# An output projection's left half ranked ahead of the last attention block, and weight casts queued behind a copy

## The chip, the cores and the metric

The kernel runs on one core of a Trainium2 chip. The metric is the device time of one execution in microseconds. The core's engines work from queues of their own: TensorE (PE, matrix products and transposes), ScalarE (ACT), VectorE (DVE), GpSimd (POOL), and SyncE (SP), from which most loads are issued.

## The reference

One decoder layer on a sequence of 1024 tokens, width 1024, in float32:

```python
z = h @ w_in                                  # columns: [pool group | q | k | v]
y_pool = pool_mixer(u_pool, w_pool, pool_scale)   # causal means over 2, 4, 8, 16 tokens, minus the token, a map per group
y_attn = sliding_window_attention(q, k, v, sinks) # window 128, 8 query heads, 2 key heads, blocks of 128 queries
mix = concat([y_pool, y_attn]) @ w_out
h = layer_norm(ALPHA * h + mix, ln1_g, ln1_b)
ff = square(relu(h @ w_ff1)) @ w_ff2
h = layer_norm(ALPHA * h + ff, ln2_g, ln2_b)
h = h + sigmoid(h @ w_ple_gate + b) * (p @ w_ple)
```

## The kernel before

Every product is made of three: each operand is split into a high part (a cast by ScalarE, `high`, L98) and a low part (the difference, `low`, L103, by VectorE or GpSimd), and `mm3` adds high x high (L112), high x low (L113) and low x high (L114) in one PSUM bank.

The tokens are worked on in two halves of 512 (t = 0, 1), in eight blocks of 128. `z_tile` makes 128 columns of z for one half. The first three (keys, values, first query) are made by `z_first`. `values` copies its product to SBUF (L238), transposes it on TensorE (L241) and splits it. `queries(t, half)` loads and splits the weights of two tiles of queries, multiplies, and evicts (L260, L261). `attention(n)` does one block: for each of the two key groups two score tiles (L288, L289, into banks of the tag "s", of which there are two), a reduction against bias and sinks by VectorE (L292), exponentials by ScalarE (L299) behind a small copy of the sinks by GpSimd (L297), the scaling (L305), transposes (L312), and products with the values (L317, L318), added up at L321. `pooling` makes the pooling groups: a product of z in a bank "mm" (three of them), its copy (L348), sums on GpSimd (L356), the difference on VectorE (L359), its split into the tile tmp, and a product with `wp` in another bank "mm", evicted at L374 and L375.

`out_left(t, ...)` multiplies the four blocks of a half with the left 512 columns of w_out: eight k steps, four blocks, three products each, 96 in all. Four accumulators are taken for all of it: three banks "mm" and one "s". The weights come in four pieces of two k steps through two tiles "w", each cast by ScalarE and, in the first half, finished by GpSimd. `residual_left` adds the accumulators to the residual (L436), which `residual_load` has fetched. `out_right(n)` does the right columns of a block, with weights kept in two large tiles, in one bank "mm".

The order in which each engine issues is not written out by hand. A planner in the framework lays out the whole program before it runs: where several instructions could go, the one that is earlier in the program goes first, by planned times; an instruction that isn't ready is passed over. `tc.issue_after(i)` puts all that is traced within it, on the engine of i, behind i. So the place of a call in the program is a rank, and not a place in time. The calls around the edits stand at L471 to L491 and L588 to L600.

Of the kernel before, what the change touches and what calls it, by code (L numbers as in the profile page):

```python
# [12 lines left out]
P = 128  # L13
D = 1024
S = 1024
HALF = 512
# [51 lines left out]
def layer(ctx, tc, xT, x, pT, w_in, w_pool, pscale, sinks, w_out, ln1, w1, w2, ln2, w_ple, w_gate, bgate, bias, rcount, out):  # L68
    nc = tc.nc
# [6 lines left out]
    def nm(s):  # L76
        uid[0] += 1
        return f"{s}_{uid[0]}"
# [4 lines left out]
    def wt(shape, dt=F32R):  # L83
        return sb.tile(shape, dt, tag="w", bufs=2, name=nm("w"))

    def nat(shape, dt=F32):
        return sb.tile(shape, dt, tag="n", bufs=8, name=nm("n"))

    def stage(shape):
        return sb.tile(shape, F32, tag="st", bufs=2, name=nm("st"))  # L90
# [5 lines left out]
    def high(dst, src, scale=None):  # L96
        if scale is None:
            nc.scalar.copy(out=dst, in_=src)  # L98
        else:
            nc.scalar.mul(out=dst, in_=src, mul=scale)  # L100

    def low(eng, dst, src, hi):
        return eng.tensor_tensor(out=dst, in0=src, in1=hi.bitcast(F32), op=ALU.subtract)  # L103
# [38 lines left out]
    def keep(shape, dt=F32R):  # L142
        return pa.tile(shape, dt, tag="k", bufs=3, name=nm("k"))
# [4 lines left out]
    def row(shape, dt=F32):  # L148
        return pa.tile(shape, dt, tag="h", bufs=6, name=nm("h"))
# [14 lines left out]
    def acc_ps():  # L164
        return ps.tile([P, HALF], F32, tag="mm", bufs=3, name=nm("mm"))

    def tr_ps():
        return ps.tile([P, 4, P], F32, tag="pt", bufs=2, name=nm("pt"))
# [13 lines left out]
    def z_tile(c, t, home=None):  # L182
        w = (home or wt)([P, 2, NK, P])
        load_split(w[:, 0], w[:, 1], w_in[c], [P, NK, P], nc.vector)
        o = acc_ps()
        for k in range(NK):
            z_mm(o, w, t, k)
        return o
# [3 lines left out]
    def z_first():  # L192
        w = [wt([P, 2, NK, P]) for _ in range(2)] + [big([P, 2, NK, P])]
        raw = [stage([P, NK, P]) for _ in range(2)]
        xr = [nat([P, 2, HALF]) for _ in range(4)]
        raw.append(nat([P, NK, P]))

        def w_part(c, a, b):
            load_split(w[c][:, 0, a:b], w[c][:, 1, a:b], w_in[c, :, a:b], None, nc.vector, raw[c][:, a:b])

        def x_part(a, b):
            d = xs[0][a // 4][:, :, a % 4 : a % 4 + b - a, :]
            load_split(d[:, 0], d[:, 1], xT[0, a // 2, :, a % 2 : a % 2 + b - a, :], None, nc.vector, xr[a // 2][:, a % 2 : a % 2 + b - a])

        for c, a, b in FIRST:
            if c < 3:
                w_part(c, a, b)
            else:
                x_part(a, b)
        os = [acc_ps() for _ in range(3)]  # L210
        for k in range(NK - 2):
            for c in range(3):
                z_mm(os[c], w[c], 0, k)
        for c in range(3):
            for k in range(NK - 2, NK):
                z_mm(os[c], w[c], 0, k)
        return os
# [16 lines left out]
    def values(t, o):  # L234
        if t == 0:
            VV[0] = keep([P, NT, 2, 2, HD])
        vt = row([P, HALF])
        nc.scalar.copy(out=vt, in_=o)  # L238
        pv = tr_ps()
        for b in range(4):  # L240
            nc.tensor.transpose(pv[:, b, :], vt[:, b * P : (b + 1) * P], ident)  # L241
        v4 = pv.rearrange("p b (g d) -> p b g d", g=2)
        dst = VV[0][:, 4 * t : 4 * t + 4]
        for g in range(2):
            high(dst[:, :, g, 0, :], v4[:, :, g, :])
            low(nc.vector, dst[:, :, g, 1, :], v4[:, :, g, :], dst[:, :, g, 0, :])

# [2 lines left out]
    def queries(t, half):  # L252
        for j in (2 * half, 2 * half + 1):
            o = first[2] if t == j == 0 else z_tile(2 + j, t, big if t == 0 and j == 1 else None)
            q = nat([P, 2, HALF], F32R)
            QQ[t][j] = q
            for i in range(2):
                r = slice(i * HD, (i + 1) * HD)
                sc = HD ** -0.5 / SLOPES[2 * j + i]
                high(q[0:HD, i, :], o[r, :], sc)  # L260
                nc.vector.scalar_tensor_tensor(  # L261
                    out=q[HD:P, i, :], in0=o[r, :], scalar=sc, in1=q[0:HD, i, :].bitcast(F32),
                    op0=ALU.mult, op1=ALU.subtract,
                )
# [72 lines left out]
    def pooling(n):  # L337
        for _ in range(n):
            while steps and len(ahead) < 2:
                gi, t = steps.pop(0)  # L340
                ahead.append((gi, t, z_tile(6 + gi, t)))
            pool_group(*ahead.pop(0))

    def pool_group(gi, t, o):
        win = WINDOWS[gi]
        u = row([P, PAD + HALF])
        nc.gpsimd.tensor_copy(out=u[:, 0:PAD], in_=halo[:, gi, :])
        nc.scalar.copy(out=u[:, PAD:], in_=o)  # L348
        if t == 0:
            nc.gpsimd.tensor_copy(out=halo[:, gi, :], in_=u[:, HALF : HALF + PAD])  # L350
        sums = [row([P, PAD + HALF]) for _ in range(2)]
        cur, a, side = 1, u, 0
        while cur < win:
            d0 = 2 * cur - 1
            b = sums[side]
            nc.gpsimd.tensor_tensor(out=b[:, d0:], in0=a[:, d0:], in1=a[:, d0 - cur : PAD + HALF - cur], op=ALU.add)  # L356
            a, side, cur = b, 1 - side, 2 * cur
        dd = sums[side][:, PAD:]
        nc.vector.scalar_tensor_tensor(  # L359
            out=dd, in0=a[:, PAD:], scalar=1.0 / win, in1=u[:, PAD:], op0=ALU.mult, op1=ALU.subtract  # L360
        )
        if t == 0:
            f = win - 1
            nc.gpsimd.tensor_tensor(out=dd[:, 0:f], in0=a[:, PAD : PAD + f], in1=rc[:, 0:f], op=ALU.mult)
            nc.gpsimd.tensor_tensor(out=dd[:, 0:f], in0=dd[:, 0:f], in1=u[:, PAD : PAD + f], op=ALU.subtract)
        dT = tmp([P, 2, HALF], F32R)
        high(dT[:, 0], dd)
        low(nc.gpsimd, dT[:, 1], dd, dT[:, 0])
        y = acc_ps()
        mm3(y, wp[:, 0, gi, :], wp[:, 1, gi, :], dT[:, 0], dT[:, 1], True, True)  # L370
        if mixP[t] is None:
            mixP[t] = big([P, 2, 4, HALF])
        m = mixP[t]
        high(m[:, 0, gi, :], y, psc[:, gi : gi + 1])  # L374
        nc.vector.scalar_tensor_tensor(  # L375
            out=m[:, 1, gi, :], in0=y, scalar=psc[:, gi : gi + 1], in1=m[:, 0, gi, :].bitcast(F32),
            op0=ALU.mult, op1=ALU.subtract,
        )
# [5 lines left out]
    first = z_first()  # L384
# [3 lines left out]
    nc.sync.dma_start(out=psc, in_=pscale)  # L388
    nc.sync.dma_start(out=rc, in_=rcount.partition_broadcast(P))
    nc.sync.dma_start(out=nd, in_=bias)  # L390
    values(0, first[1])

    hn = [None] * NT

# [31 lines left out]
    def out_load(dst, dh, kk, st, eng):  # L426
        load_split(dst[:, 0], dst[:, 1], w_out[dh, kk], None, eng, st)

    def out_mm(o, n, k, w):
        m = (mixP if k < 4 else mixA)[n // 4]  # L430
        c = (n % 4) * P
        mm3(o, m[:, 0, k % 4, c : c + P], m[:, 1, k % 4, c : c + P], w[:, 0, k % 2, :], w[:, 1, k % 2, :], k == 0, k == NK - 1)

    def residual(n, dh, o):
        v = hn[n][:, dh * HALF : (dh + 1) * HALF]
        nc.vector.scalar_tensor_tensor(out=v, in0=v, scalar=ALPHA, in1=o, op0=ALU.mult, op1=ALU.add)  # L436


    def out_left(t, staging, eng, room=None):
        blocks = range(4 * t, 4 * t + 4)  # L440
        os = [acc_ps() for _ in range(3)]
        os.append(ps.tile([P, HALF], F32, tag="s", bufs=2, name=nm("s")))
        for k in range(NK):
            if k % 2 == 0:
                w = room[:, k // 2 - 2] if room is not None and k > 3 else wt([P, 2, 2, HALF])
                out_load(w, 0, k // 2, staging(), eng)
            for n in blocks:
                out_mm(os[n % 4], n, k, w)
        return os

    def residual_load(t):
        for n in range(4 * t, 4 * t + 4):
            hn[n] = nat([P, D])
            nc.sync.dma_start(out=hn[n], in_=x[n * P : (n + 1) * P, :])

    def residual_left(t, os):
        for n in range(4 * t, 4 * t + 4):
            residual(n, 0, os[n % 4])
# [11 lines left out]

    queries(0, 0)  # L471
    load_x(1)
    queries(0, 1)
    attention(0)
    queries(1, 0)
    attention(1)
# [11 lines left out]
    pooling(2)  # L488
    attention(6)
    pooling(2)  # L490
    attention(7)  # L491
    pa_ctx.close()


# [90 lines left out]

        return rest

    residual_load(0)  # L588
    residual_left(0, out_left(0, lambda: stage([P, 2, HALF]), nc.gpsimd))
    for j in range(2):  # L590
        w = big([P, 2, 2, 2, HALF])
        for i in range(2):
# [372 lines left out]
```

## Time and profile before

| | us |
|---|---|
| median of 3 runs | 1001.99 |
| lowest, highest | 1001.53, 1002.48 |
| the profiled execution | 1001.69 |
| its span, first to last instruction | 999.9 |
| TensorE busy in the span | 989.0 |

The profile is of one execution; its span is 1.8 us shorter than its time. Times in the rows count from the start of the span. A row of a timeline merges like instructions that follow each other; the number in brackets is how long the engine stood idle before it and what ended that. The ends of TensorE's products are modelled and overlap, so the distance of two starts says more than the length of one.

### The profile page before, as it was taken

The page shows a single profiled execution, that of the slowest core. Times are in us where ns is not written, and L with a number is a line of the kernel's source. Part 1 is how long each engine was busy: PE and PEld are TensorE (multiplying, and loading weights), DVE is VectorE, ACT ScalarE, POOL GpSimd, SP SyncE. Part 2 cuts the span into 40 slices and gives each one's busy share as a digit, 9 for nine tenths or more (in the row PEclk, how much of TensorE's full clock was granted, in tenths as well). Part 3 has the DMA queues.
Part 4 walks back from the last instruction along what each step waited for, and adds up shares of the span by engine and source line. Part 5 has one row for each costly group of instructions (what it writes and reads, how often), then busy time and mean ns, then how long its engine had stood idle before and what let it go on. Part 6 is the DMA issues. An engine that isn't in the chain of part 4 may idle for free.

```text
span 999.9 us, 12215 instructions
## 1 busy us (share of the span) xinstructions
PE 989.0 (99%) x4562; PEld 821.3 (82%) x4562; DVE 708.9 (71%) x1121; ACT 458.7 (46%) x737; POOL 128.3 (13%) x158
## 2 busy tenths in 40 slices
PE   8999998999999999999999999999999999999998
PEld 7888886888888888888888888888888888888887
DVE  5788898585878776565446856887647699897333
ACT  5677767522576444344453433433433354551111
POOL 0022655520000000100000000100012010000000
PEclk9999999999999999999999999999999999999999
DMA  6524113342252533663363893675798863621011
GB/s 216 180 65 159 52 64 127 105 148 85 85 190 106 184 132 137 194 184 117 99 234 152 310 339 109 169 236 193 216 217 179 206 163 127 206 79 43 32 43 43
DMA packets 39004, 148.01 MB, mean 148 GB/s; under 512 B 4768, under 2 KB 5920, under 8 KB 36128
## 3 DMA queue, kind: packets, MB, share of 16 engines
q1 hardware_dynamic: 29952, 116.29, 33.7%
q0 software_dynamic: 7840, 26.74, 11.3%
q10 hardware_dynamic: 1152, 4.19, 1.0%
q8 instruction: 36, 0.59, 0.2%
q14 instruction: 24, 0.20, 0.1%
HBM read 124.66 MB, written 22.54 MB: 147 GB/s over the span
## 4 chain that ended last, share of the span: by engine, by line
PE 92%; DVE 3%; ACT 2%; POOL 1%; issue 1%; DMA 1%; SPq 0%; ACTq 0%; POOLq 0%; DVEq 0%
PE f L113 22%; PE f L114 22%; PE f L112 22%; PE mm L112 7%; PE mm L113 7%; PE mm L114 7%; DVE e L305 1%; PE pt L312 1%; PE f L423 1%; POOL h L356 1%; ACT e L299 1%; DMA n<-in_xT 1%; DVE pp L103 1%; PE av L318 0%; PE s L289 0%
## 5 line engine op out<-in xcount | busy, mean ns | idle before, releaser
L112 PE MATMUL f<-c,ws 128*128 128x512 f32 (+1 forms) x456 | 175.8, 385 | 0.0
L113 PE MATMUL f<-c,ws 128*128 128x512 f32 (+1 forms) x456 | 175.7, 385 | 0.0
L114 PE MATMUL f<-c,ws 128*128 128x512 f32 (+1 forms) x456 | 175.2, 385 | 0.0
L113 PE MATMUL f<-x,w 128*128 128x512 f32 x448 | 174.3, 389 | 0.0
L114 PE MATMUL f<-x,w 128*128 128x512 f32 x448 | 174.3, 389 | 0.0
L112 PE MATMUL f<-x,w 128*128 128x512 f32 x448 | 147.1, 389 | 0.0
L98 ACT CAST w<-st 128x1024 fp32r<-128x1024 f32 (+2 forms) x66 | 65.9, 999 | 108.7 <-issue 69.8
L103 DVE TENSOR_TENSOR w<-st,w 128x1024 fp32r<-128x1024 f32 (+2 forms) x62 | 73.0, 1179 | 46.6 <-ACT w L98 46.5
L112 PEld LDWEIGHTS f<-c,ws 128*128 128x128 f32 x456 | 85.7, 188 | 17.2
L113 PEld LDWEIGHTS f<-c,ws 128*128 128x128 f32 x456 | 85.7, 188 | 17.1
L114 PEld LDWEIGHTS f<-c,ws 128*128 128x128 f32 x456 | 85.7, 188 | 17.0
L113 PEld LDWEIGHTS f<-x,w 128*128 128x128 f32 x448 | 84.1, 188 | 17.6
L114 PEld LDWEIGHTS f<-x,w 128*128 128x128 f32 x448 | 84.1, 188 | 17.5
L112 PEld LDWEIGHTS f<-x,w 128*128 128x128 f32 x448 | 84.0, 188 | 17.3
L98 ACT CAST ws<-w 128x512 fp32r<-128x512 f32 x60 | 37.1, 622 | 59.3 <-PE f L114 42.4
L103 DVE TENSOR_TENSOR x<-ws,x 128x1024 fp32r<-128x1024 f32 x52 | 63.4, 1218 | 0.0
L103 DVE TENSOR_TENSOR ws<-w,ws 128x512 fp32r<-128x512 f32 x60 | 41.2, 689 | 27.4 <-ACT ws L98 27.0
L117 DVE TENSOR_TENSOR n<-t,f 128x512 f32<-128x512 f32 x48 | 31.9, 684 | 39.3 <-PE f L114 39.2
L112 PE MATMUL mm<-c,w 128*128 128x512 f32 x144 | 56.6, 398 | 0.8 <-ACT w L98 0.4
L98 ACT CAST ws<-st 128x512 fp32r<-128x512 f32 x48 | 29.8, 621 | 60.0 <-PE f L114 35.2
L113 PE MATMUL mm<-c,w 128*128 128x512 f32 x144 | 56.4, 393 | 0.3 <-DVE c L103 0.3
L114 PE MATMUL mm<-c,w 128*128 128x512 f32 x144 | 56.5, 395 | 0.0
(214 smaller groups left out, 1846.9 us busy)
## 6 DMA issues: line engine op xcount, KB each, us to landing
ws<-in_w SPq DMA_DIRECT2D x70, 512.0 KB, 3.6
w<-in_w SPq DMA_DIRECT2D x16, 1024.0 KB, 5.0
c<-fd SPq DMA_DIRECT2D x6, 2048.0 KB, 8.4
fd<-n POOLq DMA_DIRECT2D x20, 512.0 KB, 3.6
ws<-in_w POOLq DMA_DIRECT2D x20, 512.0 KB, 7.5
st<-in_w_in SPq DMA_DIRECT2D x17, 512.0 KB, 3.3
w<-in_w SPq DMA_DIRECT2D x10, 512.0 KB, 3.9
n<-in_x SPq DMA_DIRECT2D x8, 512.0 KB, 5.8
```

What stands on the lines that cost most here:

```text
L98: nc.scalar.copy(out=dst, in_=src)
L103: return eng.tensor_tensor(out=dst, in0=src, in1=hi.bitcast(F32), op=ALU.subtract)
L112: nc.tensor.matmul(o, ah, bh, start=first, stop=False, skip_group_check=more)
L113: nc.tensor.matmul(o, ah, bl, start=False, stop=False, skip_group_check=more)
L114: nc.tensor.matmul(o, al, bh, start=False, stop=last, skip_group_check=more)
L117: nc.vector.tensor_tensor(out=o, in0=a, in1=b, op=op)
L299: nc.scalar.activation(out=e[:, i, k0 : 2 * P + 1], in_=e[:, i, k0 : 2 * P + 1], func=AF.Exp, bias=st[:, i : i + 1], scale=-1.0, accum_out ...
L305: nc.vector.tensor_scalar(out=e[:, i, k0 : 2 * P], in0=e[:, i, k0 : 2 * P], scalar1=st[:, 12 + i : 13 + i], scalar2=None, op0=ALU.mult)
L312: nc.tensor.transpose(pt[:, i, :], e[:, i, kb * P : (kb + 1) * P], ident)
L356: nc.gpsimd.tensor_tensor(out=b[:, d0:], in0=a[:, d0:], in1=a[:, d0 - cur : PAD + HALF - cur], op=ALU.add)
L423: nc.tensor.transpose(pt[:, k, :], y[:, kt * P : (kt + 1) * P], ident)
```

## The change

`values` returns its copy, and the second pair of query tiles of the first half is traced behind that copy: this binds ScalarE's instructions of `queries(0, 1)`, the two weight casts and the query evictions. In the second place the loads of the residual and the left product of the first half stand in the program ahead of block 7 (the last) instead of behind it; the addition to the residual stands behind block 7.

```diff
--- before.py
+++ after.py
@@ -235,7 +235,7 @@
         if t == 0:
             VV[0] = keep([P, NT, 2, 2, HD])
         vt = row([P, HALF])
-        nc.scalar.copy(out=vt, in_=o)
+        copied = nc.scalar.copy(out=vt, in_=o)
         pv = tr_ps()
         for b in range(4):
             nc.tensor.transpose(pv[:, b, :], vt[:, b * P : (b + 1) * P], ident)
@@ -244,6 +244,7 @@
         for g in range(2):
             high(dst[:, :, g, 0, :], v4[:, :, g, :])
             low(nc.vector, dst[:, :, g, 1, :], v4[:, :, g, :], dst[:, :, g, 0, :])
+        return copied
 
 
 
@@ -388,7 +389,7 @@
     nc.sync.dma_start(out=psc, in_=pscale)
     nc.sync.dma_start(out=rc, in_=rcount.partition_broadcast(P))
     nc.sync.dma_start(out=nd, in_=bias)
-    values(0, first[1])
+    copied = values(0, first[1])
 
     hn = [None] * NT
 
@@ -470,7 +471,8 @@
 
     queries(0, 0)
     load_x(1)
-    queries(0, 1)
+    with tc.issue_after(copied.ins):
+        queries(0, 1)
     attention(0)
     queries(1, 0)
     attention(1)
@@ -488,7 +490,10 @@
     pooling(2)
     attention(6)
     pooling(2)
+    residual_load(0)
+    left = out_left(0, lambda: stage([P, 2, HALF]), nc.gpsimd)
     attention(7)
+    residual_left(0, left)
     pa_ctx.close()
 
 
@@ -585,8 +590,6 @@
 
         return rest
 
-    residual_load(0)
-    residual_left(0, out_left(0, lambda: stage([P, 2, HALF]), nc.gpsimd))
     for j in range(2):
         w = big([P, 2, 2, 2, HALF])
         for i in range(2):
```

## Rows read from the trace of the kernel before

**Rows 1.** The page: its first part, engine, busy us (share of the span), instructions; and its fourth part, the shares by engine of the chain that ended last.

```profile
PE 989.0 (99%) x4562; PEld 821.3 (82%) x4562; DVE 708.9 (71%) x1121; ACT 458.7 (46%) x737; POOL 128.3 (13%) x158
...
PE 92%; DVE 3%; ACT 2%; POOL 1%; issue 1%; DMA 1%; SPq 0%; ACTq 0%; POOLq 0%; DVEq 0%
```

**Rows 2.** Who waited for whom on TensorE, in the stretches 0 to 60, 60 to 120, 120 to 165 and 165 to 215 us: the waiting instruction, its releaser, us in total, times, longest.

```profile
PE pt L241 <- ACT h L238: 0.6, 1, 0.6
...
PE av L318 <- DVE pp L103: 0.4, 1, 0.4
...
PE mm L112 <- ACT tmp L98: 1.7, 2, 1.0
PE mm L113 <- POOL tmp L103: 0.9, 1, 0.9
...
PE av L317 <- DVE y L321: 0.7, 1, 0.7
```

**Rows 3.** Windows: the stretch, its length, busy us and instructions of each engine, the granted TensorE clock (1.00 is full), DMA share and GB/s.

```profile
160.00:165.00 5.00, 2.42 (x14) 1.47 (x12) 4.84 (x13) 4.32 (x10) 2.74 (x3) 1.00 0.66 210
165.00:170.00 5.00, 4.72 (x20) 3.75 (x20) 3.82 (x10) 3.76 (x12) 3.85 (x3) 0.66 0.51 190
...
165.00:166.00 1.00, 0.92 (x5) 0.68 (x5) 1.00 (x5) 1.00 (x3) 1.00 (x1) 1.00 0.00 0
166.00:167.00 1.00, 0.80 (x4) 0.53 (x3) 1.00 (x4) 0.41 (x1) 1.00 (x2) 0.51 0.00 0
...
200.00:220.00 20.00, 20.00 (x90) 16.57 (x89) 17.19 (x30) 6.06 (x8) 4.13 (x4) 1.00 0.53 184
```

**Rows 4.** Timelines of ScalarE and of TensorE around the copy of the values (L238) and the transposes of them (L241): start, us, engine, line, operation, out<-in, count, and in brackets the idle time before.

```profile
21.32 1.17 ACT L98 CAST k<-mm 64x512 fp32r<-64x512 f32 x2 [3.19 <-PE mm L114]
22.52 1.05 ACT L98 CAST w<-st 128x1024 fp32r<-128x1024 f32 x1
23.47 0.58 ACT L238 COPY h<-mm 128x512 f32<-128x512 f32 x1
...
22.03 0.39 PE L114 MATMUL mm<-c,w 128*128 128x512 f32 x1
22.26 0.39 PE L113 MATMUL mm<-c,c 128*128 128x512 f32 x1
...
23.16 0.39 PE L114 MATMUL mm<-c,c 128*128 128x512 f32 x1
24.10 0.66 PE L241 MATMUL pt<-ident,h 128*128 128x128 f32 x4 [0.55 <-ACT h L238]
...
30.23 0.45 PE L112 MATMUL mm<-c,w 128*128 128x512 f32 x1
```

**Rows 5.** Timelines of GpSimd, ScalarE and TensorE: the first low part of the left product's weights, the copy of the last pooling input, the last pooling group's first product, and the left and right products.

```profile
153.45 2.42 POOL L103 TENSOR_TENSOR w<-st,w 128x1024 fp32r<-128x1024 f32 x1
...
162.08 0.58 ACT L348 COPY h<-mm 128x512 f32<-128x512 f32 x1
...
170.29 0.50 PE L112 MATMUL mm<-tmp,wp 128*128 128x512 f32 x1
170.63 0.40 PE L112 MATMUL mm<-w,c 128*128 128x512 f32 x1
...
197.49 0.39 PE L112 MATMUL s<-w,c 128*128 128x512 f32 x1
...
198.85 0.39 PE L112 MATMUL mm<-c,c 128*128 128x512 f32 x1
```

**Rows 6.** Timelines of TensorE and VectorE: the first products of block 7's four score tiles, and the first reduction of the first of them.

```profile
157.90 0.28 PE L288 MATMUL s<-k,n 128*128 128x256 f32 x1
...
160.48 0.36 PE L288 MATMUL s<-k,n 128*128 128x256 f32 x1
...
165.51 0.39 PE L288 MATMUL s<-k,n 128*128 128x256 f32 x1
...
168.25 0.56 PE L288 MATMUL s<-k,n 128*128 128x256 f32 x1
...
163.68 0.47 DVE L292 CUSTOM_DVE_ANT_0 e<-s,nd,sink_sb 128x256 f32<-128x256 f32 x1
```

**Rows 7.** Timelines of VectorE, GpSimd and ScalarE: the last pooling group's difference (L359), the copy of the sinks for block 7 (L297), its first exponential, and the cast of the difference.

```profile
166.78 0.78 DVE L359 SCALAR_TENSOR_TENSOR h<-h,h 128x512 f32<-128x512 f32 x1
...
166.95 0.67 POOL L297 COPY e<-sink_sb 128x4 f32<-128x4 f32 x1
...
167.65 0.51 ACT L299 ACTIVATE e<-e,sm 128x257 f32<-128x257 f32 x1 [1.24 <-POOL e L297]
...
169.63 0.60 ACT L98 CAST tmp<-h 128x512 fp32r<-128x512 f32 x1
```

**Rows 8.** Timelines of ScalarE, TensorE and VectorE: the cast of the left product's third weights, the first of block 7's last four value products, the block's last add, the first additions of the left accumulators to the residual; and, from the view of the tile x, the first and last start of the second half's left products with its weights.

```profile
182.70 1.05 ACT L98 CAST w<-st 128x1024 fp32r<-128x1024 f32 x1 [1.65 <-PE mm L114]
...
191.37 0.39 PE L317 MATMUL av<-pp,k 128*128 128x512 f32 x1
...
194.25 0.69 DVE L321 TENSOR_TENSOR y<-av,yl 64x512 f32<-64x512 f32 x1
195.65 1.36 DVE L436 SCALAR_TENSOR_TENSOR n<-n,mm 128x512 f32<-128x512 f32 x2 [0.71 <-PE mm L114]
...
L112 PE MATMUL mm<-x,c x12: 389/389/389, 230.1 to 239.7; 128*128 128x512 f32 x12
```

## The prediction

> **What bounds the kernel now.** I read the page first. TensorE is busy 989.0 us of a span of 999.9, and 92% of the chain that ended last lies on it [rows 1]. So a microsecond counts only where TensorE stands still or runs slow. The view of the waits by stretch lists those places: 0.6 us near 24 us, for a copy by ScalarE; 0.4 us near 79 us; and between 120 and 215 us a cluster of 1.7, 0.9 and 0.7 us [rows 2]. From 200 us on the stretch I show is full [rows 3], and the waits view has no row behind 215 us. The windows then put a size on the cluster: from 160 to 165 us TensorE is busy 2.42 us of 5; from 165 to 170 us it is busy 4.72 but its granted clock is 0.66 of full, 1.00 in the microsecond from 165 and 0.51 in the next, that is 1.2 instead of 2.4 GHz, right after the thin stretch [rows 3]. The reader is to see there that both edits aim at such places: the second at 24 us, the first at 160 to 170 us. Together these hold some 7 us, so no outcome can be a large one.
>
> **The copy of the values.** At 21.32 us ScalarE casts keys; at 22.52 us it casts weights of the queries (1.05 us); only at 23.47 us it copies the values [rows 4]. But the values' last product starts at 22.03 us and its row is 0.39 us long, so at 22.42 us the copy could have begun. TensorE starts the last product of the first query at 23.16 us; products follow each other at 0.23 us (22.03, 22.26), so it is free at 23.39, and the transposes start at 24.10 with a wait of 0.55 in their row [rows 4]. With the copy first: it starts at 22.52, ends at 22.52 + 0.58 = 23.10, ahead of 23.39. The wait goes: **-0.55 us** (-0.7 by the distance 24.10 - 23.39).
>
> What is late next: the weight cast, by 0.6 us. Behind it on ScalarE stand the other weight cast and the evictions of the first query; whoever waits for the weights is the product at 30.23 us [rows 4], 7 us later, so 0.6 us is covered. If that cover were gone the cost would be the same 0.6 us. No DMA is issued in the edit; the loads of later weights wait for the staging tile, thus 0.6 us more, also inside these 7 us. Bounds: 0 (a later wait, such as that of 0.4 us near 79 us, takes the gain back) to -0.7. I take -0.55, since TensorE is full between.
>
> **The left product ahead of block 7.** Removed: nothing. The same 96 products, four weight casts on ScalarE, four low parts on GpSimd and the loads are issued, in another order of rank. The loads were issued early before already (the first weights' low part starts at 153.45 us [rows 5]), so moving them past SP's queue costs nothing; the residual loads need tiles that block 7 does not use. What rank changes follows from who gets a bank. The rows show that banks of one tag are handed out in program order: the copy of the last pooling input starts at 162.08 us and frees an "mm" bank, the weights' low part starts at 153.45, yet the first left product starts at 170.63, right behind the first product of the last pooling group at 170.29 [rows 5]. Pooling stays ahead of the left product in the program, so three of its four accumulators still begin there. The edit cannot fill the hole with them.
>
> The fourth accumulator is an "s" bank, shared with the scores. In the kernel before it came after all four score tiles of block 7, which start at 157.90, 160.48, 165.51 and 168.25 us [rows 6]. In the changed program it comes ahead of them, and needs only the first weights. That such an "s" accumulator runs ahead of its siblings is seen once already: the second half's one has products at 197.49 us, ahead of the right products that stand before it in the program and start at 198.85 [rows 5]. So two of its k steps, 2 x 3 = 6 products, can run from about 158 us: 6 x 0.23 = 1.4 us of work moves ahead of 170.3, into a stretch where TensorE idles 2.6 us of 5. Against it the scores now have one bank: the tile that started at 160.48 waits for the bank that the first tile leaves, whose reduction starts at 163.68 [rows 6], and the last tile falls behind 170.3: four products of half width, at half of 0.23 us each some 0.5 us, that must be done later. Net **-0.9 us**; bounds 0 (the 6 products only push the attention work out by as much) to -2.7 (12 products, both first weight tiles, and nothing pushed out).
>
> Third, ScalarE. The last pooling group's difference is made at 166.78 us (VectorE, 0.78 us), so its cast could start at 167.6; it starts at 169.63, behind four exponentials of block 7 that start at 167.65, after GpSimd's small copy at 166.95 [rows 7]. The whole left product hangs on that cast, through the bank. If block 7's second score tile comes a microsecond later, as just worked out, two of its exponentials (half of 169.63 - 167.65 = 1.98 us) fall behind the cast: -1.0 us. Bounds 0 to -2.0. I take **-0.8 us**, nearer the half than the whole since the order is fixed beforehand from planned times that I can't see.
>
> After 170.3 us I cost the rest at nothing: TensorE is full in both orders, because what block 7 gives up in rank the left product takes. The third weights are cast at 182.70, when two of the products' tiles are released; block 7's last value product is at 191.37 us [rows 8], the next user of its result is the second half's left product, whose k steps of attention stand behind right products and whose late weights are first used at 230.1 us [rows 8]. That cover is 30 us; block 7 may slip by 10 without being waited for.
>
> Sum: -0.55 - 0.9 - 0.8 = -2.25 us, on the profiled execution's own 1001.69: 999.4. That execution is 0.3 us under the median of the runs, 1001.99, so I state **999.6** (between 999.4 and 999.7).
>
> TensorE's clock falls behind the thin stretch [rows 3]. The Trainium skill, TensorE: Matmul & The Clock Gate, What's actually happening, says that the throttled state is the default and that activity releases it; the trace agrees (1.00, then 0.51 after 2.42 busy us of 5). By that rule fuller TensorE would keep the clock; whether six products are enough no row shows.
>
> **Rivals.**
>
> *Clock kept.* With the hole partly filled the clock stays at 2.4 GHz. From 165 to 170.3 us TensorE then needs about half of its 4.7 us, so the second pair of k steps of the fourth accumulator (1.4 us) fits in too, and the cast comes early (-2.0). -0.55 - 0.9 - 1.4 - 2.0 = -4.9: about 997. For it: the stretch is busy mostly with slow products. Against: the start of 170.3 is set by ScalarE's cast, not by TensorE. 0.14.
>
> *Only the copy.* The "s" products land in front of attention work that then lands in the hole later, at half clock, and gain nothing; the cast stays behind the exponentials. 1001.69 - 0.55 = 1001.1, about 1001.3 against the median. For it: everything that starts 170.3 belongs to pooling and keeps its rank. 0.24.
>
> *Nothing.* The planner's order stays and the 0.55 us is taken back at a later wait for VectorE or ScalarE (0.4 near 79 us, 1.7 near 150 to 162 [rows 2]): 1001.7 to 1002. 0.05.
>
> *Slower: one score bank.* Block 7 goes through one "s" bank, a round being scores (0.5) and two reductions (2 x 0.47), four rounds some 6 to 7 us instead of overlapped; its tail (value product, copy, add) then ends after the left product. VectorE evicts the left accumulators in its queue; the row of before has the block's last add at 194.25 us right in front of them at 195.65 [rows 8]. If TensorE is through with the left product while that add still waits, the right products get no bank. It decides from the point where block 7's last value product is less than about 1.5 us ahead of the end of the left product; the price is the block's remaining copy (0.58, by the copy of the values [rows 4]), add (0.69) and one eviction (0.68), 2.0 us for one key group, 4 to 5 for both: about 1005. Against: block 7 can also be evicted first, and right products need only one bank to go on. 0.12. This is where a page speaks against the change: the Trainium skill, Perfetto Trace Analysis, Optimizing Tensor Performance, says that independent groups of matmuls should rotate through different PSUM banks so that eviction overlaps the next group. No run so far shows scores on one bank.
>
> Forecast: 0.45.
>
> **How the numbers follow.** A measurement of this kernel can tell about 0.2%, 2.0 us, from no change, so the line is at 1000.0. The forecast's own range, from bounds of its terms, is -1.0 to -4.0 (998.0 to 1001.0); about two thirds of it is under 1000.0. Faster: 0.30 of the forecast, the clock rival 0.14, a little of the copy: 0.45. Slower: 0.12. The rest, 0.43, within 0.2%. The range leaves out a tenth at either end: 997.4 (short of the clock rival's end) to 1002.6 (half of the slower one is above it).
>
> **What would show it.** Right: no wait for the copy at the transposes near 23.4 us; products into an "s" bank before the last pooling group's first product; that product ahead of 169.5 us; idle from 160 to 165 us down from 2.6 to about 1.5; nothing idle at the change to the right products. Wrong: the fourth accumulator still behind the scores; or a wait of the right products' first product for VectorE's add; or an altered order between 30 and 160 us that opens new waits, which the sum does not hold, since the order is planned as a whole.

## The result and the profile after

The changed kernel takes 1004.37 us (median of 20 runs, 1003.11 to 1005.78) against 1002.18 us (20 runs, 1001.49 to 1003.66) for the kernel before on the same chip: a ratio of 1.0020 with an interval of 1.0013 to 1.0027. So it is slower by about 2.2 us where a gain of 2.25 us was forecast, and outside the range. The profiled execution took 1003.74 us with a span of 1001.9 (1001.69 and 999.9 before). In the changed kernel the lines behind L247 stand one further down: L359 of before is L360, L305 is L306, L312 is L313, L318 is L319.

The page of the changed kernel, engines and chain:

```profile
PE 989.8 (99%) x4562; PEld 822.2 (82%) x4562; DVE 709.4 (71%) x1121; ACT 459.0 (46%) x737; POOL 129.2 (13%) x158
...
PE 91%; DVE 5%; ACT 2%; POOL 1%; issue 1%; DMA 1%; SPq 0%; ACTq 0%; DVEq 0%; POOLq 0%
```

Beside [rows 1] TensorE is busy 0.8 us longer with the same 4562 instructions, and stands idle 1001.9 - 989.8 = 12.1 us instead of 999.9 - 989.0 = 10.9. Together that is the 2.0 us of the spans. VectorE's share of the chain that ended last rose from 3% to 5%.

**The copy did what it was to do.** Timelines of ScalarE and TensorE in the changed kernel, beside [rows 4]; and GpSimd's first low part of the left product's weights:

```profile
22.43 0.59 ACT L238 COPY h<-mm 128x512 f32<-128x512 f32 x1
22.91 2.00 ACT L98 CAST w<-st 128x1024 fp32r<-128x1024 f32 x2
...
23.07 0.40 PE L114 MATMUL mm<-c,c 128*128 128x512 f32 x1
23.31 0.60 PE L241 MATMUL pt<-ident,h 128*128 128x128 f32 x4
...
152.59 2.40 POOL L103 TENSOR_TENSOR w<-st,w 128x1024 fp32r<-128x1024 f32 x1
```

The copy stands ahead of both weight casts, and the transposes follow the last product without a wait (24.10 with 0.55 of idle before). At 152.59 the kernel is 0.86 us ahead of [rows 5], where the same low part starts at 153.45. All that is lost is lost behind this point. (Of the 0.86 us, 0.09 are no work of the edit: ahead of it, the product that starts at 11.70 us in the kernel before starts at 11.61; rows not shown.) Who waited for whom on TensorE from 165 to 215 us:

```profile
PE av L319 <- DVE pp L103: 2.5, 1, 2.5
PE pt L313 <- DVE e L306: 0.9, 1, 0.9
PE s L289 <- DVE sm L293: 0.4, 1, 0.4
```

All are waits for VectorE. The first kind stands in [rows 2] with 0.4 us near 79 us, and from 165 to 215 us the kernel before has 0.2 us of it (a row not shown); the other two it doesn't have. Windows of the changed kernel (columns as in [rows 3]), and behind them those of the kernel before for stretches that [rows 3] leave out:

```profile
160.00:165.00 5.00, 3.04 (x11) 1.48 (x10) 4.44 (x8) 4.32 (x9) 3.62 (x3) 0.93 0.31 105
165.00:170.00 5.00, 2.69 (x9) 2.21 (x10) 4.32 (x8) 2.28 (x5) 4.19 (x4) 0.50 0.30 105
170.00:175.00 5.00, 5.00 (x23) 4.21 (x22) 1.98 (x3) 1.74 (x5) 0.19 (x1) 0.89 0.01 3
180.00:185.00 5.00, 4.44 (x25) 3.58 (x23) 4.17 (x10) 3.51 (x7) 3.58 (x2) 1.00 0.50 165
185.00:190.00 5.00, 4.34 (x21) 3.51 (x22) 4.14 (x16) 3.16 (x10) 2.48 (x2) 1.00 0.55 207
...
164.00:165.00 1.00, 0.66 (x1) 0.19 (x1) 0.97 (x2) 1.00 (x3) 1.00 (x1) 0.66 0.57 229
```

```profile
170.00:175.00 5.00, 4.88 (x23) 3.87 (x21) 4.76 (x18) 3.86 (x12) 1.44 (x2) 1.00 0.38 129
180.00:185.00 5.00, 5.00 (x25) 4.14 (x24) 1.08 (x2) 2.79 (x4) 2.45 (x2) 1.00 0.00 0
185.00:190.00 5.00, 5.00 (x25) 4.15 (x24) 1.96 (x3) 2.19 (x5) 3.58 (x2) 1.00 0.38 131
```

The hole from 160 to 165 us is filled a little (3.04 busy instead of 2.42), as forecast. The next one opens: 2.69 busy from 165 to 170 us instead of 4.72, and all of it at a granted clock of 0.50, that is 1.2 GHz. In windows of one microsecond the mean is 0.66 from 164 us and 0.50 from 165 to 171. Between the levels 1.00 and 0.50 a mean of 0.66 says that the clock fell near 164.3 us, while the value product of 164.20 still ran: ahead of the pause that follows it until 167.31, and not by it. Before, it fell at 166 [rows 3]. A second pair of holes, 0.56 and 0.66 us, opens at 180 to 190 us, where TensorE was full.

**What happens at 164 us.** TensorE first: products of the fourth left accumulator ("s"), score tiles, value products, the last pooling group's first product.

```profile
157.05 0.39 PE L112 MATMUL s<-w,c 128*128 128x512 f32 x1
...
160.06 0.40 PE L114 MATMUL s<-w,c 128*128 128x512 f32 x1
160.29 0.28 PE L289 MATMUL s<-k,n 128*128 128x256 f32 x1
...
164.20 0.66 PE L318 MATMUL av<-pp,k 128*128 128x512 f32 x1 [0.45 <-DVE y L322]
167.31 0.79 PE L319 MATMUL av<-pp,k 128*128 128x512 f32 x1 [2.46 <-DVE pp L103]
...
171.94 0.39 PE L112 MATMUL mm<-tmp,wp 128*128 128x512 f32 x1
...
174.90 0.28 PE L289 MATMUL s<-k,n 128*128 128x256 f32 x1
```

The "s" products do come ahead, six of them from 157.05 to 160.06. Block 7's second score tile, however, starts at 174.90 instead of 160.48 [rows 6]. And the last pooling group's first product, the one that was to come earlier, is at 171.94 instead of 170.29 [rows 5], with no wait in its row: it simply stands behind other products. The value product at 167.31 had waited 2.46 us for VectorE's low part. Here is VectorE around it, with GpSimd and ScalarE:

```profile
163.76 2.35 POOL L103 TENSOR_TENSOR w<-st,w 128x1024 fp32r<-128x1024 f32 x1
...
164.08 2.58 DVE L360 SCALAR_TENSOR_TENSOR h<-h,h 128x512 f32<-128x512 f32 x1
166.58 1.27 DVE L103 TENSOR_TENSOR pp<-pt,pp 128x512 fp32r<-128x512 f32 x2
167.78 0.47 DVE L293 CUSTOM_DVE_ANT_0 e<-s,nd,sink_sb 128x256 f32<-128x256 f32 x1
...
166.69 0.62 ACT L98 CAST tmp<-h 128x512 fp32r<-128x512 f32 x1 [1.15 <-DVE h L360]
```

The difference of the last pooling group (L360) took 2.58 us; in [rows 7] the same line took 0.78. It started 0.32 us after GpSimd's low part of the second weights, and ended at 164.08 + 2.58 = 166.66, that is 0.55 us after that low part's end (163.76 + 2.35 = 166.11). In the kernel before, the two met as well, but only at the tail. GpSimd's low part there:

```profile
164.64 2.37 POOL L103 TENSOR_TENSOR w<-st,w 128x1024 fp32r<-128x1024 f32 x1
```

It ended at 167.01; the difference, 166.78 and 0.78 long [rows 7], ended at 167.56, again 0.55 us after it. Before, block 7's first reductions stood ahead of the difference in VectorE's queue (the first at 163.68 [rows 6]) and filled the time of GpSimd's low part. In the changed kernel the first of them stands behind it, at 167.78.

The theory, then: the change takes one of two "s" banks from block 7's scores; its reductions leave VectorE's queue ahead of the difference; so the difference meets GpSimd's whole low part, is held until that ends, and the low parts of block 6's probabilities and the value product wait behind it. The rival: one score bank is by itself what costs, scores and reductions going one after the other.

### The profile page after: what moved, and what is told of

Read it like the earlier page. It is cut to its first block, busy times and chain, and to the rows that moved or that the text cites. A ratio compares the mean times of both kernels' runs of the same rounds, so it can differ in the third digit from the quotient of the medians.

```text
span 1001.9 us, 12220 instructions
## 1 busy us (share of the span) xinstructions
PE 989.8 (99%) x4562; PEld 822.2 (82%) x4562; DVE 709.4 (71%) x1121; ACT 459.0 (46%) x737; POOL 129.2 (13%) x158
## 4 chain that ended last, share of the span: by engine, by line
PE 91%; DVE 5%; ACT 2%; POOL 1%; issue 1%; DMA 1%; SPq 0%; ACTq 0%; DVEq 0%; POOLq 0%
PE f L112 22%; PE f L114 22%; PE f L113 22%; PE mm L113 6%; PE mm L114 6%; PE mm L112 6%; DVE e L306 1%; PE pt L313 1%; PE f L424 1%; DVE e L293 1%; DVE pp L103 1%; POOL h L357 1%; PE av L319 1%; DMA n<-in_xT 1%; DVE h L360 1%
```

## The experiments

**The two edits apart.** e1 has the copy alone (`values` returns it, as in the change):

```diff
+    copied = values(0, first[1])
...
+    with tc.issue_after(copied.ins):
+        queries(0, 1)
```

> The second edit alone: the kernel before, with the first half's second pair of query tiles traced behind the copy of the values; the left product stays behind block 7. Theory (the copy gains, the move loses): the transposes of the values start near 23.3 us without a wait, TensorE is 0.9 us ahead of the kernel before at 157 us, the stretch from 160 to 170 us looks as before, and the time is 0.6 to 0.9 us under the kernel before. Rival (the copy's edit upsets the planned order and is the loss): 1 us or more over the kernel before, with new waits behind 100 us.

1001.33 us against 1002.07; ratio 0.9994 (0.9985 to 1.0002). The time alone can't tell this from nothing; its trace can. The product that starts at 11.70 us before starts at 11.97 in e1, 0.27 us late ahead of the edit, and the value product near 79 us starts at 78.26 instead of 78.74, 0.48 us early (rows not shown): 0.75 us for the copy. In the changed kernel the same two rows, 11.61 and 77.89, give 0.76. e2 has the move alone:

> The first edit alone: the left product ahead of block 7, the weight casts as in the kernel before. Theory (the move is the whole loss): about 2.9 us over the kernel before, 1005, with the wait of some 2.5 us of a value product near 165 us and those of transposes and scores near 185 us. Rival (the loss comes only with both edits, since the copy shifts one engine against the other): within 1 us of the kernel before, no wait over 1 us at 165.

1005.24 us; ratio 1.0029 (1.0018 to 1.0040): 3.2 us slower, with the same three waits. Its granted clock is 0.82 from 165 to 170 us and 0.84 from 170 to 175 (0.50 and 0.89 in the change), so TensorE ran slow for half as long, and e2 loses no less than the change: the loss is not made by the longer low clock of the change. VectorE and GpSimd of e2 at the meeting:

```profile
165.46 2.58 DVE L360 SCALAR_TENSOR_TENSOR h<-h,h 128x512 f32<-128x512 f32 x1
...
165.14 2.35 POOL L103 TENSOR_TENSOR w<-st,w 128x1024 fp32r<-128x1024 f32 x1
```

The whole loss belongs to the move. -0.74 + 3.17 = +2.4 is about what both together cost (+2.2).

**Through which bank?** e5 has the copy, and e6 both edits, with the fourth block's left product of the first half left out of the computation, so that no "s" bank is taken:

```diff
-        blocks = range(4 * t, 4 * t + 4)
+        blocks = range(4 * t, 4 * t + 3 + t)
...
-        os.append(ps.tile([P, HALF], F32, tag="s", bufs=2, name=nm("s")))
+        if t:
+            os.append(ps.tile([P, HALF], F32, tag="s", bufs=2, name=nm("s")))
...
```

> The second edit alone, and the fourth block's left product of the first half left out (24 of 96 products, its bank of the scores' tag and its addition to the residual), so that part of the computation is missing. It is the base for the next kernel. All theories: 24 products at 0.227 us, 5.4 us, under the second edit alone: about 996.

> Both edits, with the same fourth block's left product left out: the left product is ahead of block 7 but takes no bank of the scores' tag. Theory (the move acts through that bank alone: it puts products ahead of the scores, and makes the scores share the other bank): the first score tile of block 7 starts right behind the last pooling input again, the waits near 185 us are gone, and the time is within 0.8 us of the kernel without the move. Rival (the rank on ScalarE, GpSimd and VectorE does the harm by itself): 1.5 to 3 us over it, with the pooling difference of over 2 us again.

996.56 and 996.51 us, the same ratio of 0.9945 (0.9933 to 0.9958) for both. Without the fourth accumulator the move is worth nothing, in either direction. VectorE and GpSimd of e6, which has the move:

```profile
165.36 0.47 DVE L293 CUSTOM_DVE_ANT_0 e<-s,nd,sink_sb 128x256 f32<-128x256 f32 x1
165.76 0.78 DVE L360 SCALAR_TENSOR_TENSOR h<-h,h 128x512 f32<-128x512 f32 x1
...
163.61 2.38 POOL L103 TENSOR_TENSOR w<-st,w 128x1024 fp32r<-128x1024 f32 x1
```

The reductions stand ahead of the difference again, and the difference is held at its tail only (165.76 + 0.78 = 166.54, 0.55 after GpSimd's 165.99). e8 keeps all the work and both edits but puts the fourth accumulator into a bank of the transposes:

```diff
-        os.append(ps.tile([P, HALF], F32, tag="s", bufs=2, name=nm("s")))
+        os.append(tr_ps().rearrange("p a b -> p (a b)") if t == 0 else ps.tile(...))
```

> Both edits, with the fourth accumulator of the first left product in a bank of the transposes' tag instead of the scores'; block 7's scores keep two banks, its transposes have one. Theory (two causes: the meeting near 165 us and scores on one bank near 185 us): the waits of scores near 185 us are gone, the four score tiles start before 172 us; whether the time falls by their 1.3 us hangs on the transposes, which then wait for casts of 0.6 us and low parts of 0.7 us each: between 1 us under and 1 us over the changed kernel. Rival (scores on one bank are the main loss): 2 us or more under the changed kernel.

1001.88 us; ratio 0.9998 (0.9989 to 1.0007), 2.4 us better than the change by the distances to the kernel before. TensorE's waits from 120 to 165 us are those of before, and the long ones behind 165 us are gone. With the gain of the early products goes the loss as well (the fourth accumulator's first product comes at 176.44 us, a row not shown): both hang on the "s" bank. The expectation's theory, within 1 us of the change, was missed, and the number is what its rival gave, 2 us or more for scores on one bank. But e8 takes the meeting away together with the one bank (its difference takes 0.77 us), so it can't part the two.

**The meeting, or the one bank?** e7 keeps both edits and the one score bank, and only queues GpSimd's second low part behind the last pooling group's own low part, so that it starts after the difference:

```diff
+        lowp.append(low(nc.gpsimd, dT[:, 1], dd, dT[:, 0]))
...
+                if t == 0 and k == 2:
+                    with tc.issue_after(lowp[-1].ins):
+                        out_load(w, 0, k // 2, staging(), eng)
...
```

> Both edits; of the first left product's weights the second piece's low part, still on GpSimd, is queued behind the last pooling group's low part. Nothing else is edited. Theory (GpSimd's 2.35 us low part beside VectorE's last pooling difference is the loss near 165 us): the difference takes about 0.7 us instead of 2.58, the value product's wait of 2.5 us is under 0.8 us, TensorE's clock is low for 4 us or less, and the time is 1.5 to 3.5 us under the changed kernel, 1001 to 1003. Rival (what made the version with VectorE's low parts fast is another planned order, or less work on GpSimd, and not this meeting): within 0.7 us of the changed kernel's 1004.4, or a new wait as long at another place.

1000.66 us; ratio 0.9983 (0.9974 to 0.9991): 3.6 us better than the change, more than expected. VectorE, GpSimd and TensorE of e7, where the difference is L361:

```profile
164.24 0.69 DVE L361 SCALAR_TENSOR_TENSOR h<-h,h 128x512 f32<-128x512 f32 x1
164.85 1.28 DVE L103 TENSOR_TENSOR pp<-pt,pp 128x512 fp32r<-128x512 f32 x2
...
173.27 1.14 DVE L306 TENSOR_SCALAR e<-e,sm 128x256 f32<-128x256 f32 x4
...
167.67 2.39 POOL L103 TENSOR_TENSOR w<-st,w 128x1024 fp32r<-128x1024 f32 x1
...
165.59 0.50 PE L319 MATMUL av<-pp,k 128*128 128x512 f32 x1 [0.76 <-DVE pp L103]
```

With the same place in VectorE's queue the difference takes 0.69 us instead of 2.58, and the value product waits 0.76 us instead of 2.46. The holes at 180 to 190 us are gone as well (TensorE is busy 5.00 us in both windows), though the scores still have one bank. In the changed kernel they have the same origin as the first one. VectorE, GpSimd and TensorE of the changed kernel there:

```profile
181.94 3.30 DVE L306 TENSOR_SCALAR e<-e,sm 128x256 f32<-128x256 f32 x4
185.16 0.47 DVE L293 CUSTOM_DVE_ANT_0 e<-s,nd,sink_sb 128x256 f32<-128x256 f32 x1
...
182.72 4.76 POOL L103 TENSOR_TENSOR w<-st,w 128x1024 fp32r<-128x1024 f32 x2 [0.65 <-ACT w L98]
...
185.30 0.44 PE L313 MATMUL pt<-ident,e 128*128 128x128 f32 x2 [0.86 <-DVE e L306]
186.10 0.39 PE L289 MATMUL s<-k,n 128*128 128x256 f32 x1 [0.37 <-DVE sm L293]
```

Block 7, pushed back, has its scalings (four of L306, 1.14 us in e7) just where GpSimd makes the third weights' low part: they take 3.30 us, the transposes wait for them, and the reduction behind them is late for the one score bank. One bank adds the last 0.37 us; the 0.86 and the lateness come from a second meeting. In e7 the scalings are done at 174.4, long before GpSimd's next low part at 181.41.

An estimate from the traces parts the loss. Sum over TensorE's products by how much the distance from one start to the next exceeds the pace of full stretches (0.23 us at 512 columns, 0.12 at 256, 0.06 for a transpose); this holds waits and slow clock alike, to about 0.2 us, a product at either end:

| us lost by TensorE | e1, the copy alone | the change | e7 | e10 (below) |
|---|---|---|---|---|
| 60 to 176 us | 15.3 | 16.4 | 14.4 | 15.4 |
| 176 to 206 us | 0.8 | 2.6 | 1.1 | 2.1 |

So of the 2.9 us that the move costs, about 1.1 are lost up to 176 us and 1.8 behind it: the stretch of the second meeting weighs more than that of the first.

e12 turns the question round: the kernel before, no edit of the change, and only the reductions of block 7's second tile (first key group) queued behind the difference:

```diff
+                    with (tc.issue_after(diffs[0].ins) if n == 7 and g == 0 and j == 1 else ExitStack()):
+                        nc.vector.tensor_tensor_reduce(
...
+        diffs[0] = nc.vector.scalar_tensor_tensor(
```

> The kernel before, without either edit; only the reductions of block 7's second score tile are queued behind the last pooling difference on VectorE, which is what one bank for the scores did in the changed kernel. Theory (the difference, two operands in SBUF, is held while GpSimd makes a low part, and the reductions, which read PSUM, are not): the difference starts near 165.5 us, beside the low part that ends near 167, and takes 1.5 to 2 us instead of 0.78, ending at 167.6 as before; the time is within 1 us of the kernel before, since it ends no later. Rival (the 2.58 us of the changed kernel come from something else in it, such as TensorE's accumulating bank): the difference takes 0.7 to 0.8 us, ends at 166.4, and the last pooling group's cast and product come a microsecond earlier.

```profile
166.06 1.58 DVE L361 SCALAR_TENSOR_TENSOR h<-h,h 128x512 f32<-128x512 f32 x1
...
164.72 2.38 POOL L103 TENSOR_TENSOR w<-st,w 128x1024 fp32r<-128x1024 f32 x1
```

The meeting comes about with no left product near it: 1.58 us, to 167.64, 0.54 us after GpSimd's end at 167.10. The time, 1001.50 us, ratio 0.9991 (0.9982 to 1.0000), shows no loss: there the difference was issued 0.72 us earlier than in [rows 7] and held 0.80 us longer, so that it ended only 0.08 us later. So the holding is shown apart from the change. Its cost is not: that rests on e7, e10 and e3, which take the low part out of the way.

**The low parts off GpSimd.** e3 has both edits and the four low parts on VectorE:

```diff
-    left = out_left(0, lambda: stage([P, 2, HALF]), nc.gpsimd)
+    left = out_left(0, lambda: stage([P, 2, HALF]), nc.vector)
```

> Both edits, and the four low parts of the first left product's weights made by VectorE instead of GpSimd. Theory (the wait near 165 us is VectorE held by GpSimd's 2.35 us low part: one difference of 128 x 512 took 2.58 us instead of 0.67): the difference takes about 0.7 us again, the value product's wait of 2.5 us is under 0.7 us, the clock is low for at most 4 us instead of 7, and the time is 1 to 2.5 us under the changed kernel; the waits near 185 us, from scores on one bank, stay at 1 us or more. Rival (scores on one bank are the whole loss): the time stays within 0.5 us of the changed kernel.

997.59 us; ratio 0.9952 (0.9940 to 0.9964): 4.5 us faster than the kernel before and the fastest that does all the work. Against the change that is 6.7 us where 1 to 2.5 were expected, and the waits near 185 us, which were to stay, are gone too. Its windows, and its VectorE and TensorE:

```profile
160.00:165.00 5.00, 3.81 (x22) 2.93 (x21) 4.94 (x9) 4.00 (x8) 2.08 (x3) 1.00 0.21 59
165.00:170.00 5.00, 5.00 (x26) 4.15 (x25) 3.02 (x8) 3.15 (x8) 2.08 (x3) 1.00 0.39 154
```

```profile
161.75 1.21 DVE L103 TENSOR_TENSOR w<-st,w 128x1024 fp32r<-128x1024 f32 x1
162.88 0.68 DVE L360 SCALAR_TENSOR_TENSOR h<-h,h 128x512 f32<-128x512 f32 x1
...
164.64 0.48 PE L112 MATMUL mm<-tmp,wp 128*128 128x512 f32 x1
```

VectorE makes a low part in 1.21 us where GpSimd takes 2.35, the difference takes 0.68, the last pooling group begins at 164.64 instead of 171.94, and the clock stays at 1.00. That is about the price of the prediction's rival "clock kept", by another door. Part of it is a meeting that the kernel before has already. Four of its scalings stand beside the first low part of [rows 5]:

```profile
154.48 3.13 DVE L305 TENSOR_SCALAR e<-e,sm 128x256 f32<-128x256 f32 x4
```

In e3 they take 0.60 us a pair. How much of the 4.5 us each of the meetings holds is not parted. e9 is e3 without the copy edit:

> The first edit alone, with the first left product's four low parts on VectorE, and the weight casts as in the kernel before. Theory (the copy's edit is worth 0.7 to 0.9 us in any of these versions, the move with the lows off GpSimd the other 3.7): 0.5 to 1 us over the version that has both edits and the lows on VectorE, so 998.1 to 998.6. Rival (the edits work together, since the copy shifts one engine against the other): 2 us or more over it, or no difference.

998.19 us; ratio 0.9958 (0.9945 to 0.9970): the copy is worth about 0.6 us here too. e4 is the copy and the low parts on VectorE without the move:

> The second edit alone, with the first left product's low parts on VectorE, the left product behind block 7. Theory (GpSimd's low parts hold VectorE in the kernel before too: four scalings near 154 us took 3.1 us where others take 1.1): the scalings take 1.1 to 1.4 us, the pooling chain is earlier, and the time is 1.5 to 3 us under the kernel before. Rival (VectorE has 4 x 1.2 us more to do just where its queue is full): no better than the second edit alone, or up to 2 us worse.

1001.04 us; ratio 0.9991 (0.9981 to 1.0001), so hardly more than the copy alone, where 1.5 to 3 us were expected. One row of its TensorE and one of its VectorE tell why no more comes of it:

```profile
165.09 1.08 PE L313 MATMUL pt<-ident,e 128*128 128x128 f32 x4 [4.00 <-DVE pp L103]
...
162.12 1.21 DVE L103 TENSOR_TENSOR w<-st,w 128x1024 fp32r<-128x1024 f32 x1
```

VectorE's queue is free of GpSimd there, but full: it is busy 4.93 us from 160 to 165 us, as the expectation's rival had it, TensorE waits 4.00 us at one place, and no "s" product stands there. Why the planner orders it so is not visible. So the move is worth +2.2 + 0.7 = +2.9 us with the low parts on GpSimd (the change against e1) and -4.5 + 1.0 = -3.5 us with them on VectorE (e3 against e4), by the distances to the kernel before.

e10 and e11 put one of the four low parts on VectorE, e10 the second (as shown), e11 the first (`k == 0` in place of `k == 2`):

```diff
-                out_load(w, 0, k // 2, staging(), eng)
+                out_load(w, 0, k // 2, staging(), nc.vector if t == 0 and k == 2 else eng)
```

> Both edits, and of the four low parts of the first left product's weights only the second is made by VectorE. Theory (the second low part's meeting with the last pooling difference near 165 us is the larger loss): the difference takes 0.7 us, the wait of 2.5 us is under 1 us, and the time is 2.5 to 4 us under the changed kernel, near the version that queues that part later (1000.7). Rival (the first low part, near 153 us, is what delays the stretch): the time stays within 1 us of the changed kernel.

> Both edits, and of the four low parts only the first is made by VectorE. Theory (the first part holds VectorE's four scalings near 154 us, 3.1 us instead of 1.2, and so everything behind them): the scalings take 1.2 to 1.5 us, the pooling differences come 1.5 to 2 us earlier, so that the second part on GpSimd may or may not meet the last one; 1 to 5 us under the changed kernel, with the larger gain if it does not. Rival (the scalings have slack): within 0.7 us of the changed kernel, the meeting with the last difference as before.

e10: 1001.03 us, ratio 0.9987 (0.9978 to 0.9996), 3.3 us better than the change; the first meeting is gone (0.69 for the difference), the second remains (scalings of 3.28 us near 181 us), and TensorE waits 1.2 us for VectorE's low part. Its trace is of an execution of 1002.42 us and has the clock at 0.50 in all of 165 to 170 us, like the change; the 15.4 us above hold that too. e11: 1001.90 us, ratio 1.0001 (0.9991 to 1.0010), 2.4 us better. Without the first low part on GpSimd the four scalings near 155 us take 1.2 us, all runs earlier, and the second low part meets another instruction. VectorE and GpSimd of e11:

```profile
160.80 4.05 DVE L306 TENSOR_SCALAR e<-e,sm 128x256 f32<-128x256 f32 x4
...
162.30 2.39 POOL L103 TENSOR_TENSOR w<-st,w 128x1024 fp32r<-128x1024 f32 x1
```

Four scalings took 4.05 us, and TensorE waited 3.3 us behind them. Near 181 us the scalings take 3.30 us here too. A meeting moves with the order; what gets rid of it is a low part off GpSimd, or at a time when VectorE has nothing of that kind.

## Why the prediction was wrong, step by step

**The copy: right.** The wait of 0.55 us went and the cover held. The two traces give 0.75 us, a little over the bound of 0.7, the two pairs of runs 0.7 and 0.6.

**The "s" products ahead: right in kind.** Six products came from 157.05 to 160.06, and TensorE's idle time from 160 to 165 us fell from 2.58 to 1.96 us. Whether the term of -0.9 would have stood with nothing else moved, no run shows by itself; in e7 TensorE lost 0.9 us less than in e1 up to 176 us, where this term and the next make 1.7.

**The third term: the step that failed.** It said "if block 7's second score tile comes a microsecond later". It came 14.4 us later (174.90 for 160.48 [rows 6]). What followed on ScalarE was even better than forecast: the cast of the difference at 166.69 instead of 169.63 [rows 7], 2.9 us earlier against a bound of 2.0. But the term followed the late tile on ScalarE alone. On VectorE the same lateness took the reductions from ahead of the difference, and the difference then ran into GpSimd's low part: +1.9 us on it and 2.46 us of wait on the value product. Up to 176 us the move lost 1.1 us by the estimate above, where this term and the one before it had 1.7 us of gain. (The low clock of 165 to 170 us, 0.50 where [rows 3] have 0.66, is not the meeting's work: it fell ahead of the pause, and e10 has it without this meeting.) The earlier cast was of no use, since the last pooling group's product had been put behind 12 "s" products and block 6's value products in TensorE's order: the start at 170.29 was no longer set by ScalarE. A sign lay in [rows 7]: a difference of 0.78 us, where the same line at 160.80 us, in a row not shown, takes 0.67. A larger one lay in the same trace: the scalings of 154.48 us, 3.13 us long, where those of 174.94 take 1.14.

**"After 170.3 us nothing": the other step that failed, by some 1.8 us.** The cover of 30 us for block 7's result held, but the block's own steps were not asked whom they would meet in their new place: 0.86 and 0.37 us of wait near 185 us. By the estimate another half microsecond is lost up to 206 us, among the steps of block 7 that had been put off; no wait in the trace names its cause. So the term that stood at nothing failed by 1.8, and the two before it, -1.7 together, by 2.8.

**The rival "one score bank"** had the right sign and the right root, block 7's scores on one bank, but its place was wrong: no right product waits for VectorE's add, and scores waited 0.37 us for their bank, where the rival had counted 2.0 us for a key group. e7, with one bank and 1.4 us faster than the kernel before, shows that the bank alone doesn't decide. The rule cited there from the Trainium skill, Perfetto Trace Analysis, Optimizing Tensor Performance, on rotating banks, thus shows here as 0.37 us of waiting for a bank, and the price of the rival was too high.

**What the sum would have needed** is a term for VectorE's instructions whose place against GpSimd's changes. The Trainium skill, SBUF — State Buffer, Who interferes with whom, states it: a VectorE instruction with two SBUF inputs contends with a GpSimd instruction that reads SBUF, and whichever of the two starts second is blocked until the first is done. The trace agrees in five kernels (ends 0.54 to 0.55 us behind GpSimd's, above). The difference has two inputs in SBUF; the reductions and the low parts of the probabilities, with one operand in PSUM, run through: the reduction at 185.16 us took 0.47 in the midst of GpSimd's 4.76, and in the kernel before a low part of the probabilities at 165.78 us took 0.69 beside GpSimd's of 164.64 (a row not shown).

Two things stay open. How much of the loss each meeting makes is known by estimate alone, 1.1 us up to 176 us and 1.8 behind: e7 removes both, e10 the first, and each alters the order too. And by which planned times the planner put tile and pooling product so far back can't be read from a trace.

## What to carry to other kernels

When a change moves an engine's queue, list for each moved stretch which VectorE instructions now stand beside GpSimd work, and read the row of any that is longer than its like: a few tenths too long are the tail of a meeting that another order can make whole. A bank taken from a tag doesn't only delay who wants it; ask what its consumers had been covering on each engine. And test an edit with the suspected neighbour off the way before giving it up: here the same move is worth +2.9 or -3.5 us by the engine of four small subtractions.

## What the runs showed of the hardware that was not expected

A held VectorE instruction is not slowed but stopped: started, by its row, 0.23 us (the kernel before, e6), 1.04 us (e12) or 2.03 us (e2, the change) before the end of GpSimd's low part, the difference ends 0.54 to 0.55 us after it each time, nearly its whole unhindered 0.67 to 0.69 us. The fp32 scalings (L306), with one tensor input in SBUF, are held too: 3.30 and 4.05 us for four instead of 1.14, ending at 185.24 in the change and 164.85 in e11, 0.14 to 0.16 us after GpSimd's low part (the first of the two, at half of 4.76 us, and 164.69). In the other direction GpSimd's copy of the sinks, 128 x 4 elements, takes 0.67 us where it overlaps the difference as that at last runs [rows 7], and 0.18 us in e7, where it doesn't (163.91 us, a row not shown). In e10 the same copy took 1.18 us, to 165.22, beside a low part that VectorE made until 165.17 (rows not shown).
